# Attention scores of a hybrid decoder layer: four fp32 products of a unit replaced by twelve fp32r products of high and low parts

## The chip, the cores and the metric

One core of one Trainium2 chip runs the kernel. TensorE (PE) multiplies, VectorE (DVE), ScalarE (ACT) and GpSimd (POOL) work on the results, and SyncE's queue (SP) issues most of the DMAs. The metric is the device time of one execution in microseconds, the median of several. The kernel before took 817.43 us (3 runs, 816.8 to 818.87).

An fp32r operand is a 32-bit number that PE reads in one pass with fewer bits than fp32. The kernel gets nearly the whole precision back with a split: a number is high part plus low part, both fp32r, and a product a·b becomes the three products high·high, high·low and low·high, added up in PSUM.

## What is computed

One layer of a decoder with two branches, an mLSTM (a matrix memory, chunk by chunk) and an attention over a sliding window with sinks, for a prompt of 1024 positions and for 8 × 4 sample positions, at a width of 1024. The change is about the scores of the prompt's attention: 8 query heads in 4 groups share 2 key heads of 64 dimensions; each block of 128 positions sees its own block and the one before it.

```python
def attn_prompt(q, k, v, sinks):
    nb = T // WINDOW                                  # 8 blocks of 128
    qb = q.reshape(B, nb, WINDOW, A_HEADS, A_HEAD_DIM)
    ...
    return sink_attend(qb, with_prev(k), with_prev(v), pos, k_pos, sinks)

def sink_attend(q, k, v, q_pos, k_pos, sinks):
    s = jnp.einsum('bnqkgd,bnskd->bnkgqs', qg, k) * (A_HEAD_DIM ** -0.5)
    ...
    mx = jnp.maximum(jnp.max(s, axis=-1, keepdims=True), sink)
    p = jnp.exp(s - mx)
    den = jnp.sum(p, axis=-1, keepdims=True) + jnp.exp(sink - mx)
    o = jnp.einsum('bnkgqs,bnskd->bnqkgd', p / den, v)

def layer(...):
    (mq, mk, mv, mi, mf, mo, mz, aq, ak, av, az, gm, ga) = split_in(h @ w_in)
    y_m, C, n, m = mlstm_branch(mq, mk, mv, mi, mf, mo, mz, C0, n0, m0, b_i, b_f, g_mn)
    q, k = partial_rope(aq, pos), partial_rope(ak, pos)
    y_a = attn(q, k, av, sinks) * jax.nn.silu(az)
    u = jax.nn.sigmoid(gm) * (y_m @ w_mo) + jax.nn.sigmoid(ga) * (y_a @ w_ao)
    x = x + gate * (u @ w_o)
```

## The kernel before

The kernel goes through the layer in stages. After the norm and the split of h into high and low parts come the projections of keys, values and queries (products g_ak, g_av, g_aq, up to 125 us), then the mLSTM's heads and the gates in blocked products (bx, bw, by, bz: twelve fp32r steps of 512 columns to a block, from the high and low parts of the activations and of the weights wh and wl), then the output projections (g_w_mo, g_w_ao, foX, foY, foW).

Between the steps of these large products a planner, the class `Side`, puts the smaller work: generators in named streams, among them "a" (the attention's units), "x" (extra work, one after the other), "s" (samples) and "g" (the gates of the mLSTM). Each `yield lag, banks` of a generator says how many planned microseconds must pass before its next part and which PSUM banks that part takes. The planner's clock `now` is moved on by `mm` with each product (the matmul itself is the helper's line L292 in the profile, transposes are L297), and a bank of the pools "b" and "o" counts as taken for 3.5 and 5.5 planned us; both pools have 2 buffers. What comes out is a fixed order of PE's, DVE's and ACT's instructions (`in_order`), so any engine that waits holds up all that stands behind. DMAs go through `dma` and `store` to SP's queue (L277), in the order in which the planner reaches them; a store with `by=S` goes to ACT's queue. A tile of `ht` is one of 49 buffers of 128 × 512 numbers.

A query group's projection ends in `ev_q`, which scales a piece of 384 or 288 columns out of PSUM on ACT (aq), rotates it for group 0 and stores it to qD in DRAM. The rotated keys stand in kD, the values in vdD.

`unit(g, b0)`, 16 times (4 groups, two blocks each), is the attention. It loads the queries of two blocks into uqv (128 × 256: the two key heads' 64 rows lie one above the other) and three blocks of keys into ukv (two at b0 = 0), waits 10.0 planned us, and multiplies: for each block i and each key head a product of 64 rows, the two heads on different halves of PE's rows, into sc_.._0 (pool "o") and sc_.._1 (pool "b"). DVE adds the mask and takes the maximum in four pieces (p, mx; the custom operations of the profile), then ACT exponentiates, DVE normalises, PE transposes (pt, pool "b"), multiplies with the values (oT, pool "b"), and ACT copies oT to ukv, from where it is stored to oD.

Three other pieces of work stand near the first unit. `smp` (pool "b") are the products of the samples with raw weights wr_mv and wr_mq, as soon as these are loaded. `fp` (pool "b") is a transpose in `gates`, the chain that makes the decays nmd and wid. `ow` are the rows of w_out times the gates ogb, which are stored back to DRAM for the output projection. `sum_blocks` in stream "x" forms the sums t2, t3 and t4 of the blocks of h that the blocked products take.

Of the kernel before, what the change touches and what calls it, by code (L numbers as in the profile page):

```python
# [20 lines left out]
D = 1024  # L21
# [167 lines left out]
def body(tc, a):  # L189
    nc = tc.nc  # L190
    with ExitStack() as ctx:
# [17 lines left out]
        def ht(shape, name, dt=F32):  # L209
            return sp.tile(shape, dt, tag="half", bufs=49, name=name)  # L210
# [49 lines left out]
        def dma(out, in_, late=False):  # L260
            stores(in_.tensor)
            issue(out, in_, late)
# [25 lines left out]
        def mm(out, lhsT, rhs, start, stop, share=1, more=False):  # L288
            n = int(np.prod(rhs.shape[1:]))
            side.now += max(n, 250) / 2400 if rhs.dtype == F32R else max(n * 4 // share, 128) / 2400  # L290
            side.products += 1
            in_order(nc.tensor.matmul(out, lhsT, rhs, start=start, stop=stop, skip_group_check=more))  # L292
# [543 lines left out]
        def unit(g, b0):  # L836
            sink = at["sink"]
            los = [128 if b == 0 else 0 for b in (b0, b0 + 1)]
            n0 = 1 if b0 == 0 else 0
            qv, kv_ = ht([128, 4, 128], "uqv"), ht([128, 4, 128], "ukv")  # L840
            q, kT = qv[:, 0:2].rearrange("p c e -> p (c e)"), kv_[:, 0:3].rearrange("p c e -> p (c e)")
# [60 lines left out]
        def queries(g):  # L902

            def ev_q(p, acc, c0, n):
                q = ht([128, 384], "aq")[:, :n]
                S.activation(q, acc[:, :n], AF.Copy, scale=0.125)
                if g == 0:
                    r = ht([128, 384], "aqr")[:, :n]
                    rope(q, at["ropeq"][p], n, r, shuf16)
                    q = r  # L910
                store(qD.rearrange("g k r s -> (g k) r s")[:, 16 * g:16 * g + 16, c0:c0 + n], q)

            job(("aq", g), ev_q)

        def sample_attention():
# [12 lines left out]
            for kv, r in enumerate(half_rows):  # L928
                dma(qsm[r], qD[:, kv, :, SEQ:T].rearrange("g r s -> r g s"))
            yield 12.0, "b"  # L930
# [386 lines left out]
        def block_split(t, hi, lo):  # L1317
            S.copy(hi, t)
            V.tensor_tensor(lo, t, hi.bitcast(F32), op=ALU.subtract)

        def sum_blocks():
# [460 lines left out]
        next(work)  # L1782
        for g in range(4):
            for b0 in (0, 2, 4, 6):
                side.add("a", unit(g, b0))
# [363 lines left out]
```

## Time and profile before

| | before |
|---|---|
| median of the runs shown | 817.43 us (816.8 to 818.87, 3 runs) |
| the profiled execution | 816.73 us |
| its span on the core | 814.9 us |
| mean granted clock of TensorE | 0.998 |
| DMA, mean over the span | 193 GB/s, 157.26 MB |
| first and last query piece leave PSUM (ACT, aq) | 72.0 and 123.0 us |
| scores of the first unit | 139.1 us |
| scores of the first unit of the second group | 185.9 us |

The profile is of one execution; the page gives each engine's busy time, the chain of work that ended last and the costliest groups. In a row of a timeline stand the start, the time until the end of the last of the group, engine, line, operation, output and inputs, the tile's shape, how many, and in brackets the idle time before and what ended it. Matmuls are pipelined: the record of one is longer than the time after which the next one starts, so what a product costs PE is read from start to start.

### The profile page before, as it was taken

How to read it: one execution, taken by the hardware profiler on the slowest of the kernel's cores; microseconds unless marked ns; L12 is line 12 of the kernel's file. 1: busy time of each engine (PE TensorE's matmuls, PEld its weight loads, DVE VectorE, ACT ScalarE, POOL GpSimd, SP SyncE). 2: the span in 40 equal slices, each digit the busy share in tenths (PEclk: the TensorE clock that was granted, in tenths of full speed). 3: DMA queues.
4: the chain of work that ended last, by engine and by line, in shares of the span. 5: the costliest groups of instructions: out<-in, count | busy, mean ns of one | idle time of the engine just before them, and what ended most of it. 6: DMA issues, size and time to landing. Idle time of an engine off the chain costs nothing.

```text
span 814.9 us, 15087 instructions
## 1 busy us (share of the span) xinstructions
PE 795.6 (98%) x5071; PEld 650.3 (80%) x5071; DVE 601.2 (74%) x1631; ACT 409.2 (50%) x996; POOL 105.3 (13%) x196
## 2 busy tenths in 40 slices
PE   6899999999999999999999999999999999999996
PEld 2688887777777767887888888787788999997785
DVE  3789747989776866665766787899786677767576
ACT  4674243655646757645454655564545244215344
POOL 0220000222222220010211110111101100000041
PEclk9999999999999999999999999999999999999999
DMA  9977646878785475744364675573455698534532
GB/s 322 373 228 203 177 125 223 265 228 238 249 249 168 115 220 171 226 135 150 101 184 133 184 188 172 160 210 91 138 169 185 227 346 305 173 102 167 204 110 104
DMA packets 111041, 157.26 MB, mean 193 GB/s; under 512 B 19712, under 2 KB 61440, under 8 KB 110932
## 3 DMA queue, kind: packets, MB, share of 16 engines
q1 hardware_dynamic: 96148, 135.58, 52.5%
q10 hardware_dynamic: 11232, 14.42, 5.0%
q0 software_dynamic: 3584, 6.30, 3.9%
q8 instruction: 40, 0.66, 0.4%
q14 instruction: 37, 0.30, 0.1%
HBM read 112.58 MB, written 44.69 MB: 193 GB/s over the span
## 4 chain that ended last, share of the span: by engine, by line
PE 93%; DVE 2%; DMA 2%; ACT 1%; issue 1%; SPq 0%; ACTq 0%; DVEq 0%
PE bw L292 14%; PE by L292 13%; PE bx L292 13%; PE bz L292 7%; PE g_aq L292 6%; PE g_w_mo L292 6%; PE g_w_ao L292 5%; PE foX L292 3%; PE foW L292 2%; PE smp L292 2%; PE foY L292 2%; PE sc L292 2%; PE oT L292 2%; PE n L292 2%; PE g_ak L292 1%; PE g_av L292 1%
## 5 line engine op out<-in xcount | busy, mean ns | idle before, releaser
L273 POOL DMA_DIRECT2D yhD<-yt x48 | 28.8, 607 | 230.9 <-DVE yt L235 139.6
L292 PE MATMUL g_w_ao<-ya,wh_w_ao 128*128 128x384 f32 (+1 forms) x192 | 45.7, 322 | 0.1
L292 PE MATMUL g_w_mo<-ym_l,wh_w_mo 128*128 128x384 f32 (+1 forms) x192 | 45.7, 323 | 0.0
L235 ACT ACTIVATE p<-p,nmx 128x256 f32<-128x256 f32 (+1 forms) x64 | 31.0, 486 | 21.4 <-DVE nmx L235 20.7
L273 POOL DMA_DIRECT2D mkN<-mkt x32 | 20.9, 659 | 133.5 <-DVE p L235 71.8
L292 PEld LDWEIGHTS g_w_ao<-ya,wh_w_ao 128*128 128x128 f32 x192 | 33.5, 188 | 0.7 <-DVE ya L235 0.6
L292 PEld LDWEIGHTS g_w_mo<-ym_l,wh_w_mo 128*128 128x128 f32 x192 | 33.5, 188 | 0.0
L292 PE MATMUL g_aq<-h_h,wh_aq 128*128 128x384 f32 (+1 forms) x96 | 31.9, 333 | 0.0
L292 PE MATMUL g_aq<-h_l,wh_aq 128*128 128x384 f32 (+1 forms) x96 | 31.0, 323 | 0.0
L292 PE MATMUL g_w_mo<-ym_l,wl_w_mo 128*128 128x384 f32 (+1 forms) x96 | 31.0, 323 | 0.0
L292 PE MATMUL g_aq<-h_h,wl_aq 128*128 128x384 f32 (+1 forms) x96 | 31.0, 323 | 0.0
L292 PE MATMUL g_w_ao<-ya,wl_w_ao 128*128 128x384 f32 (+1 forms) x96 | 30.8, 321 | 0.0
L235 ACT CAST uwh<-u_h 128x512 fp32r<-128x512 f32 x27 | 16.6, 620 | 27.3 <-PE foY L292 10.5
L235 DVE TENSOR_TENSOR uwl<-u_h,uwh 128x512 fp32r<-128x512 f32 x27 | 18.5, 689 | 12.5 <-ACT uwh L235 12.4
L235 DVE CUSTOM_DVE_ANT_0 p<-sc,cst,sink 128x256 f32<-128x256 f32 (+1 forms) x64 | 26.1, 461 | 1.0 <-PE sc L292 1.0
L273 POOL DMA_DIRECT2D mvN<-mvt x32 | 20.7, 653 | 37.3 <-DVE mvt L235 36.3
L235 ACT CAST wo_h<-wo_l 128x512 fp32r<-128x512 f32 x28 | 17.1, 620 | 13.8 <-DVE u_h L235 10.6
L235 POOL TENSOR_TENSOR fr_w<-fr_y 128x2 f32<-128x2 f32 (+1 forms) x12 | 3.5, 291 | 144.2 <-DVE fr_y L235 143.6
L235 ACT ACTIVATE p<-p,den 128x128 f32<-128x128 f32 x56 | 18.6, 394 | 5.1 <-DVE den L235 4.5
L235 DVE TENSOR_TENSOR wo_l<-wo_l,wo_h 128x512 fp32r<-128x512 f32 x28 | 18.7, 686 | 2.5 <-ACT wo_h L235 2.4
L235 DVE SCALAR_TENSOR_TENSOR p<-p,den 128x128 f32<-128x128 f32 x56 | 17.3, 345 | 4.2 <-ACT wh_pgate__3658 L235 2.9
L292 PEld LDWEIGHTS g_aq<-h_h,wh_aq 128*128 128x128 f32 x96 | 18.0, 188 | 2.7 <-issue 2.5
(1621 smaller groups left out, 2684.3 us busy)
## 6 DMA issues: line engine op xcount, KB each, us to landing
x<-xT SPq DMA_DIRECT2D x16, 256.0 KB
early_h<-w_ada SPq DMA_DIRECT2D x8, 512.0 KB
adar_ga<-w_ada SPq DMA_DIRECT2D x16, 256.0 KB
ow<-w_out SPq DMA_DIRECT2D x16, 256.0 KB
woD_t<-ow SPq DMA_DIRECT2D x16, 256.0 KB
wr_ga<-w SPq DMA_DIRECT2D x16, 256.0 KB
wr_gm<-w SPq DMA_DIRECT2D x16, 256.0 KB
taD<-gt ACTq DMA_DIRECT2D x16, 256.0 KB
```

Of the source, the lines that this page charges most:

```text
L235: ins = f(*args, **kw)
L273: nc.gpsimd.dma_start(out, in_)
L292: in_order(nc.tensor.matmul(out, lhsT, rhs, start=start, stop=stop, skip_group_check=more))
```

## The change

The queries leave PSUM in two parts: ACT writes the high part (fp32r), DVE the difference; for group 0 both are taken after the rotation. They are stored to qhD and qlD, and the 32 sample columns, unsplit, to qsD, from where `sample_attention` reads them. A new generator `key_parts` in stream "x" loads the rotated keys from kD once, splits them and stores khD and klD. `unit` loads four pieces in place of two (queries high and low into one uqv, keys into ukh and ukl), passes them through ACT in three copies in place that give them the type fp32r, and forms each block's scores from three products; the output goes to a part of p. The lag of 10.0 before the scores becomes 8.0 and, after the copies, 2.5. `sum_blocks` begins with a yield of 6.0, and the planner's cost of an fp32r product is divided by its share.

```diff
-            side.now += max(n, 250) / 2400 if rhs.dtype == F32R else max(n * 4 // share, 128) / 2400
+            side.now += max(n, 250) / share / 2400 if rhs.dtype == F32R else max(n * 4 // share, 128) / 2400
...
-        qD = dp.tile([4, 2, 64, T], F32, name="qD")
+        qD = [dp.tile([4, 2, 64, SEQ], F32, name=f"q{x}D") for x in "hl"]
+        qsD = dp.tile([4, 2, 64, NS], F32, name="qsD")
+        ksD = [dp.tile([128, SEQ], F32, name=f"k{x}D") for x in "hl"]
...
         def unit(g, b0):
-            qv, kv_ = ht([128, 4, 128], "uqv"), ht([128, 4, 128], "ukv")
-            q, kT = qv[:, 0:2]..., kv_[:, 0:3]...
-            dma(q, qD[g].rearrange("k r s -> (k r) s")[:, b0 * 128:b0 * 128 + 256])
-            dma(kT[:, n0 * 128:], kD[:, (b0 - 1 + n0) * 128:(b0 + 2) * 128])
-            yield 10.0, "obt"
+            qv = ht([128, 4, 128], "uqv", F32R)
+            q = [qv[:, 2 * i:2 * i + 2].rearrange("p c e -> p (c e)") for i in range(2)]
+            kT = [ht([128, 512], f"uk{x}", F32R)[:, :384] for x in "hl"]
+            for t, d in zip(q, qD):
+                dma(t.bitcast(F32), d[g].rearrange("k r s -> (k r) s")[:, b0 * 128:b0 * 128 + 256])
+            for t, d in zip(kT, ksD):
+                dma(t[:, n0 * 128:].bitcast(F32), d[:, (b0 - 1 + n0) * 128:(b0 + 2) * 128])
+            yield 8.0, ""
+            for t in (qv, kT[0][:, n0 * 128:], kT[1][:, n0 * 128:]):
+                S.copy(t, t.bitcast(F32))
+            yield 2.5, "obt"
...
-                for kv, r in enumerate(half_rows):
-                    mm(scs[kv][:, i, lo:], q[r, qc], kT[r, kc], start=True, stop=True, share=2)
+                for j, (x, y) in enumerate(((0, 0), (0, 1), (1, 0))):
+                    for kv, r in enumerate(half_rows):
+                        mm(scs[kv][:, i, lo:], q[x][r, qc], kT[y][r, kc], start=(j == 0), stop=(j == 2), share=2)
...
-            o = kv_[:, 0:2].rearrange("p c e -> p (c e)")
+            o = p[0][:, 0]
...
             def ev_q(p, acc, c0, n):
-                q = ht([128, 384], "aq")[:, :n]
-                S.activation(q, acc[:, :n], AF.Copy, scale=0.125)
+                parts = [ht([128, 384], f"aq{x}", F32R)[:, :n] for x in "hl"]
+                hi, lo = parts
                 if g == 0:
...
+                    rope(t, at["ropeq"][p], n, q, shuf16)
+                    S.copy(hi, q)
+                    V.tensor_tensor(lo, q, hi.bitcast(F32), op=ALU.subtract)
+                else:
+                    S.activation(hi, acc[:, :n], AF.Copy, scale=0.125)
+                    V.scalar_tensor_tensor(lo, acc[:, :n], 0.125, hi.bitcast(F32), op0=ALU.mult, op1=ALU.subtract)
...
+        def key_parts():
+            raw, hi, lo = ([ht([128, 512], f"ks{x}", dt) for _ in range(2)] for x, dt in ...)
+            for i in range(2):
+                dma(raw[i], kD[:, HALF[i]])
+            yield 6.0, ""
+            for i in range(2):
+                block_split(raw[i], hi[i], lo[i])
+                for t, d in zip((hi[i], lo[i]), ksD):
+                    store(d[:, HALF[i]], t.bitcast(F32))
+                yield 2.0, ""
+
         def sum_blocks():
...
+            yield 6.0, ""
...
         for g in (1, 0, 2):
             queries(g)
+        side.add("x", key_parts())
```

Since the planner sets the order, all work after about 130 us is laid out anew. Two places are shown.

The first is the first unit. PE, in the kernel before, where the sample products end and the unit's scores follow (by and bx are blocked products of the heads, wh and wl their weights):

```order
L292 MATMUL smp<-wr_mq_0_1512,c_106 32x128
L292 MATMUL smp<-wr_mq_1_1514,c_106 32x128
L292 MATMUL sc_0_0_1650<-ukv,uqv 128x128
L292 MATMUL sc_0_1_1651<-ukv,uqv 128x128
L292 MATMUL sc_0_0_1650<-ukv,uqv 128x256
L292 MATMUL sc_0_1_1651<-ukv,uqv 128x256
L292 MATMUL bx<-h_h_388,wh_phead_in_1__1579 128x512
```

The same engine and place after the change, from the last of the unit's scores on:

```order
L292 MATMUL sc_0_1_1710<-ukl,uqv 128x256
L292 MATMUL sc_0_0_1709<-ukh,uqv 128x256
L292 MATMUL sc_0_1_1710<-ukh,uqv 128x256
L297 MATMUL fp<-cst,gt_1120 128x32
L292 MATMUL by<-t3h_1482,wh_phead_in_7__1631 128x512
L292 MATMUL by<-t3l_1483,wh_phead_in_7__1631 128x512
L292 MATMUL by<-t3h_1482,wl_phead_in_7__1632 128x512
L292 MATMUL smp<-wr_mv_0_1574,c_106 32x128
```

The sixteen smp products stood ahead of the scores and now stand behind them, behind fp and behind three steps of by that were ahead of smp before.

DVE at this place, in the kernel before: the products of w_out's rows with the gates, one sum of raw weights, and the first of the unit's four pieces.

```order
L235 TENSOR_TENSOR ow_1536<-ow_1536,ogb_1532 128x512
L235 TENSOR_TENSOR ow_1538<-ow_1538,ogb_1533 128x512
L235 TENSOR_TENSOR ow_1540<-ow_1540,ogb_1532 128x512
L235 TENSOR_TENSOR wr_mq_0_1512<-wr_mv_0_1508,wr_mq_0_1512 128x512
L235 TENSOR_TENSOR ow_1542<-ow_1542,ogb_1533 128x512
L235 ISA p_1647,mx<-sc_0_0_1650,cst,sink 128x128
```

After the change:

```order
L235 TENSOR_TENSOR ow_1604<-ow_1604,ogb_1600 128x512
L235 TENSOR_TENSOR t4l_1620<-x_7_86,t4h_1619 128x512
L235 TENSOR_TENSOR ow_1606<-ow_1606,ogb_1601 128x512
L235 TENSOR_TENSOR ow_1608<-ow_1608,ogb_1600 128x512
L235 TENSOR_TENSOR ow_1610<-ow_1610,ogb_1601 128x512
L235 ISA p_1706,mx<-sc_0_0_1709,cst,sink 128x128
```

Four products ow and one other operation stand ahead of the pieces in both; the other one is now the low part of a sum (t4l), and the sum of raw weights comes behind the pieces. On SP's queue the loads of ow come after the weights wr_mv and wr_mq in both orders. Between them stood one load of ogb; now the loads of the low queries, of both parts of the keys and of two ogb stand there.

The second place is the unit sc_4 of the last group, at 301 to 306 us in the trace. DVE in the kernel before, from the multiplication of the decays et to the unit's first piece:

```order
L235 TENSOR_TENSOR et<-et,cst 128x384
L235 SCALAR_TENSOR_TENSOR p_3458<-p_3459,den 128x128
L235 TENSOR_TENSOR wl_pgate_3__3618<-wr_ga_1_3085,wh_pgate_3__3617 128x512
L235 TENSOR_TENSOR wl_pgate_4__3659<-wr_gm_1_3089,wh_pgate_4__3658 128x512
L235 TENSOR_TENSOR wr_gm_0_3439<-wr_ga_0_3435,wr_gm_0_3439 128x512
L235 TENSOR_TENSOR qw<-qw,hq_0_3547 128x384
L235 TENSOR_TENSOR wr_ga_0_3435<-ws_3612,wr_ga_0_3435 128x512
L235 ISA p_3596,mx<-sc_4_0_3599,cst,sink 128x256
```

After the change:

```order
L235 MEMSET hv_0_3824 128x3
L235 SCALAR_TENSOR_TENSOR p_3736<-p_3737,den 128x128 x2
L235 TENSOR_TENSOR et<-et,cst 128x384
L235 TENSOR_TENSOR wr_gm_0_3694<-wr_ga_0_3690,wr_gm_0_3694 128x512
L235 TENSOR_TENSOR wl_pgate_3__3903<-wr_ga_1_3306,wh_pgate_3__3902 128x512
L235 ISA p_3873,mx<-sc_4_0_3876,cst,sink 128x256
```

One wl, qw and the second sum of raw weights (wr_ga) now come behind the pieces.

More of the change, by code (lines that the diff above doesn't have):

```diff
@@ L902, in queries @@
         def queries(g):
+            rows = [d.rearrange("g k r s -> (g k) r s")[:, 16 * g:16 * g + 16] for d in (*qD, qsD)]
             def ev_q(p, acc, c0, n):
[L905 to L906 removed]
+                parts = [ht([128, 384], f"aq{x}", F32R)[:, :n] for x in "hl"]
+                hi, lo = parts
+                m = min(n, SEQ - c0)
                 if g == 0:
[L908 to L911, printed above, removed]
+                    q, t = (ht([128, 384], f"aqr{x}")[:, :n] for x in "qt")
+                    S.activation(t, acc[:, :n], AF.Copy, scale=0.125)
+                    rope(t, at["ropeq"][p], n, q, shuf16)
+                    S.copy(hi, q)
+                    V.tensor_tensor(lo, q, hi.bitcast(F32), op=ALU.subtract)
+                    tail = q[:, m:]
+                else:
+                    S.activation(hi, acc[:, :n], AF.Copy, scale=0.125)
+                    V.scalar_tensor_tensor(lo, acc[:, :n], 0.125, hi.bitcast(F32), op0=ALU.mult, op1=ALU.subtract)
+                    if m < n:
+                        tail = sm([128, NS], "aqs", 2)
+                        S.activation(tail, acc[:, m:n], AF.Copy, scale=0.125)
+                for t, d in zip(parts, rows):
+                    store(d[:, :, c0:c0 + m], t[:, :m].bitcast(F32))
+                if m < n:
+                    store(rows[2], tail)
             job(("aq", g), ev_q)
@@ L1319, in block_split @@
             V.tensor_tensor(lo, t, hi.bitcast(F32), op=ALU.subtract)
+        def key_parts():
+            raw, hi, lo = ([ht([128, 512], f"ks{x}", dt) for _ in range(2)] for x, dt in (("r", F32), ("h", F32R), ("l", F32R)))
+            for i in range(2):
[6 more added lines that the diff above has]
+                yield 2.0, ""
         def sum_blocks():
@@ L1782, in body @@
         next(work)
+        assert not side.streams["x"]["wait"] and len(side.streams["x"]["live"]) < 2
         for g in range(4):
```

4 lines of the change are left out of this document (2 added, 2 removed).

## The prediction

> **What bounds the kernel now.** The page comes first: who is busy, and what the chain that ended last is made of. Then the list of all the waits of TensorE (PE).
>
> ```profile
> span 814.9 us, 15087 instructions
> ...
> PE 795.6 (98%) x5071; PEld 650.3 (80%) x5071; DVE 601.2 (74%) x1631; ACT 409.2 (50%) x996; POOL 105.3 (13%) x196
> ...
> PE 93%; DVE 2%; DMA 2%; ACT 1%; issue 1%; SPq 0%; ACTq 0%; DVEq 0%
> ```
>
> ```profile
> PE xc L292 <- ACT xsq L235: 5.8, 1, 5.8
> PE pt L297 <- DVE mx L235: 2.3, 1, 2.3
> PE adat_q L292 <- ACT adas_q L235: 1.5, 2, 0.8
> PE xc L292 <- ACT xsum L235: 0.7, 1, 0.7
> PE bw L292 <- ACT bw L235: 0.7, 1, 0.7
> PE g_av L292 <- DVE wl_av L235: 0.6, 1, 0.6
> PE g_ak L292 <- DVE h_l L235: 0.5, 1, 0.5
> ```
>
> PE is busy for 98% of the span and makes up 93% of the chain. The list (us in all, times, longest) has seven kinds of wait, 12 us together, and one of them lies in the attention: 2.3 us, in which PE's transposes of the probabilities (pt) wait for VectorE (DVE). So a microsecond taken from PE's instruction stream between 137 and 310 us is a microsecond of the end, and so is each new wait of PE there; work on ScalarE (ACT), DVE or the queues costs something only where it makes PE wait.
>
> All sums below are made against the profiled execution, 816.73 us (span 814.9). The median of the runs shown is 817.43, 0.70 above it; I add that at the end. About 0.3%, 2.5 us, is what a measurement of this kernel can tell from no change: 815.0 to 819.9.
>
> **The scores (12 products for 4).** What one unit costs PE is read from start to start in PE's timeline, for the two kinds of unit.
>
> ```profile
> 175.32 0.40 PE L292 MATMUL bw<-h_h,wl_phead_in__2009 128*128 128x512 f32 x1
> 175.64 1.13 PE L292 MATMUL sc<-ukv,uqv 64*128 64x256 f32 x8
> 176.71 0.66 PE L297 MATMUL pt<-cst,p 128*128 128x128 f32 x4
> ```
>
> ```profile
> 137.78 0.39 PE L292 MATMUL by<-t3h,wl_phead_in__1559 128*128 128x512 f32 x1
> 138.10 0.30 PE L292 MATMUL smp<-wr_mv,c 128*32 128x128 f32 x2
> ...
> 139.11 0.93 PE L292 MATMUL sc<-ukv,uqv 64*128 64x128 f32 x8
> 139.96 0.50 PE L292 MATMUL bx<-h_h,wh_phead_in__1579 128*128 128x512 f32 x1
> ```
>
> A unit of two full blocks takes 176.71 − 175.64 = 1.07 us, a first unit of a group (its first block has 128 keys) 139.96 − 139.11 = 0.85. The eight records of a unit are four matmuls in two passes, and the two matmuls of a pair lie in different halves of the rows, so there are four pair passes, two for each block. The two kinds differ by 0.22 in two passes of 128 columns, 0.11 each; a pass of 256 is then 0.22, the four 0.87, and 0.20 is left for going into and out of the half-height tiles. What an fp32r step of 256 columns takes, the end of the kernel shows.
>
> ```profile
> 802.00 0.28 PE L292 MATMUL foY<-wo_h,uwh 128*128 128x256 f32 x1
> ...
> 807.63 0.28 PE L292 MATMUL foY<-wo_h,uwl 128*128 128x256 f32 x1
> ```
>
> These are 48 rows: (807.63 − 802.00) / 47 = 0.120 us a step. Six pair steps are 0.72 instead of 0.87: **−0.15 us in each of 12 units, −1.8 us**. An fp32r step of 128 columns on half the rows stands nowhere; it lies between 0.06 (half of 0.12) and 0.12 (no cheaper than 256 columns), so a first unit's six steps are 3 × 0.06 to 3 × 0.12 and 3 × 0.12, 0.54 to 0.72, where its four passes were 0.65; I take 0 for the four. The 0.20 of overhead I keep. An fp32r product on 96 rows passes without any (0.23 a step on both sides of it),
>
> ```profile
> 596.27 0.40 PE L292 MATMUL sU<-vm,skn 96*128 96x512 f32 x1
> 596.50 0.40 PE L292 MATMUL bw<-t2h,wh_phead_gate__7130 128*128 128x512 f32 x1
> ```
>
> so the overhead's bounds are 0 and 0.20, and the scores' term lies between −1.8 and −1.8 − 16 × 0.20 = −5.0; I stay near the 64-row rows, since they are the same tiles. If the two halves ran in turn, the twelve steps would be 1.44: a rival, below.
>
> The Trainium skill (TensorEngine Tiling (Array Packing), Instruction Overhead) gives each matmul about 60 cycles of overhead on this chip and advises against tiling what is already small, which speaks against more and shorter products; with the 2.4 GHz of its page TensorE: Matmul & The Clock Gate that would be an estimated 25 ns a step, some 0.05 us for the two added steps of a unit and about 1 us for the kernel. The 256-column steps above show 120 ns, only 13 above 256 such cycles, so the trace bears out about half of it, and that half is in the 0.72 already.
>
> **A new wait at the first unit.** The order of PE changes at about 138 us: the first unit's scores, the transposes fp and one block's three products now come ahead of the sample products smp, where smp came before the scores. The half of the scores on the second key head (sc_0_1), fp and smp share a pool of two banks, so smp now takes the bank of sc_0_1 and waits until DVE has read it. When that is, DVE's timeline tells.
>
> ```profile
> 137.56 2.04 DVE L235 TENSOR_TENSOR ow<-ow,ogb 128x512 f32<-128x512 f32 x3 [0.95 <-DMA ow<-w_out]
> 139.52 0.69 DVE L235 TENSOR_TENSOR wr_mq<-wr_mv,wr_mq 128x512 f32<-128x512 f32 x1
> 140.12 0.69 DVE L235 TENSOR_TENSOR ow<-ow,ogb 128x512 f32<-128x512 f32 x1
> 140.73 0.35 DVE L235 CUSTOM_DVE_ANT_0 p<-sc,cst,sink 128x128 f32<-128x128 f32 x1
> ...
> 142.08 0.09 DVE L235 DVE_READ_ACCUMULATOR2_ANT mx<- 128x1 f32 x1
> 142.95 0.24 PE L297 MATMUL fp<-cst,gt 32*128 32x32 f32 x1
> ```
>
> The reads end at 142.17, and nothing of PE waits for them now. In the new order PE gets to smp at 138.10 (where it stood) + 0.85 (the scores) + about 0.35 (fp, 0.24 and the change of tiles) = 139.3; the three products are moved, not added. That leaves 142.17 − 139.3 = **2.9 us of wait**. Behind smp in PE's queue stands everything, so it goes to the end in full. And DVE gets there later: its pieces p still stand behind four products ow and one more operation of 0.69 us, and the ow loads now stand on SP's queue behind 512 KB more since the weights (a second ogb, and the new low parts of queries and keys). At the rate of that stretch,
>
> ```profile
> 125.00:140.00 15.00, 14.34 (x97) 11.01 (x96) 10.13 (x24) 6.82 (x16) 0.00 (x0) 1.00 0.75 249
> 140.00:180.00 40.00, 40.00 (x238) 30.67 (x237) 36.57 (x109) 21.75 (x62) 9.90 (x16) 1.00 0.79 249
> 180.00:220.00 40.00, 40.00 (x276) 30.83 (x275) 31.54 (x87) 24.83 (x73) 10.98 (x18) 1.00 0.84 250
> ...
> 260.00:310.00 50.00, 47.74 (x338) 36.09 (x338) 35.51 (x114) 33.98 (x108) 10.33 (x16) 1.00 0.57 171
> ```
>
> 249 GB/s (the last column; ahead of it the DMA share, the clock and the busy times of PE, its loads, DVE, ACT and POOL), this is 2.1 us. DVE was itself waiting 0.95 us for ow there, so a later landing is not hidden. I take half: **+4.0**; the ends are +2.0 (the loads land in time and the pieces move up by the 0.95 us) and +5.5 (all of the 2.1, and one more operation of DVE ahead).
>
> **The wait at 306 us.** Before pt, DVE works through a row of 0.6 us products that begin with a late load.
>
> ```profile
> 300.98 0.56 DVE L235 TENSOR_TENSOR et<-et,cst 128x384 f32<-128x384 f32 x1 [1.06 <-DMA et<-nmd]
> ...
> 302.32 0.69 DVE L235 TENSOR_TENSOR wl_pgate__3659<-wr_gm,wh_pgate__3658 128x512 fp32r<-128x512 f32 x1
> ...
> 303.52 0.55 DVE L235 TENSOR_TENSOR qw<-qw,hq 128x384 f32<-128x384 f32 x1
> ...
> 306.35 0.66 PE L297 MATMUL pt<-cst,p 128*128 128x128 f32 x4 [2.26 <-DVE mx L235]
> ```
>
> In the new order three of them (a wl, qw and a wr_ga, 0.6 us each) come behind the pieces that lead to pt. That is 1.8 of the 2.26 us; but pt's place on PE moves too, and the load of et sits on the same queue with more ahead of it. I take **−1.2**, ends −2.3 and 0.
>
> **ACT, DVE and the queues.** Each unit adds three casts on ACT; each query piece adds a product on DVE.
>
> ```profile
> L235 ACT CAST h_h<-x 128x512 fp32r<-128x512 f32 x12 | 7.1, 621 | 0.3
> L235 ACT CAST ya<-yr 128x384 fp32r<-128x384 f32 x8 | 3.9, 508 | 0.0
> L235 DVE SCALAR_TENSOR_TENSOR u_h<-tgw_ao,g_w_ao 128x384 f32<-128x384 f32 x16 | 8.7, 550 | 6.2 <-PE g_w_ao L292 6.1
> 100.00:125.00 25.00, 25.00 (x184) 22.05 (x183) 10.76 (x25) 9.61 (x20) 0.00 (x0) 1.00 0.39 107
> ```
>
> A unit costs ACT 0.62 + 2 × 0.51 = 1.64 us, 16 units 26 us, in a stretch of 185 us where it was busy for 108 (the sum of the windows; 68% in the last, 260 to 310). The cover is ACT's idle 40%, and the unit's lag before the scores (8.0 + 2.5 planned microseconds for 10.0). Twelve query pieces are 12 × 0.55 = 6.6 us of DVE, half of them in 100 to 125, where it is idle for 14 of 25; key_parts adds two casts (1.2) and two subtractions (1.4) there. Bytes: 16 units × 320 KB, 1.5 MB for key_parts, and 2 MB of query stores, some 8.5 MB where the DMA share is 0.39 to 0.84. Where this cover is gone PE waits; I take **+0.4**, ends 0 and +4.
>
> **Sum**: 816.73 − 1.8 + 4.0 − 1.2 + 0.4 = 818.1, and 0.7 for the median: 818.8; I take off 0.2, since the unknown overhead of the tiles can only fall: **818.6**, by this sum no change that can be told.
>
> **The rivals.**
>
> *The wait stays short and the tile change shrinks.* For it: sU's step without overhead, and DVE's idle 0.95 us. Scores −4.0 (two thirds of the overhead gone), smp +2.0, pt −2.0, nothing else: 817.43 − 4.0 = 813.4. Against it: the 0.20 is measured on these very tiles, and the reads by DVE do end at 142.17. The Trainium skill (TensorEngine Tiling (Array Packing), Key Properties) says that changing the tiling mode drains TensorE; by that rule the overhead stays, and the rows of sc agree with 0.20 us, while sU at 96 rows shows none.
>
> *ACT becomes late (slower).* One mechanism: ACT runs in order, and 1.64 us of casts stand ahead of its next evacuation of a product block. In 260 to 310 four units bring 6.6 us to 33.98, 81% of the stretch. A block's twelve steps take 12 × 0.23 = 2.8 us, and with two banks PE waits as soon as ACT is later than that. For it: the wait bw <- ACT bw, 0.7 us, is of this kind. Against it: ACT's idle time there is still 9 us. Where each of the four costs 1 us: +4 on the forecast, 822.5.
>
> *The pairs run in turn.* The scores then don't get cheaper: 1.44 − 0.87 = +0.57 in 12 units, 6.8, and in the others, between 1.1 and 1.4 for 0.65, +0.6 in 4, 2.4: together +9.2 where the sum has −1.8. That is 11 on the forecast, of which 0.6 shortens the wait at smp: about 829. For it: no fp32r pair on half-height tiles stands in the trace. Against it: the fp32 pairs, in the same tiles, do run side by side.
>
> **How the numbers follow.** Forecast 0.48 (its own range 816.5 to 821), shorter wait 0.26 (813.4, ± 2), ACT late 0.16 (822.5, ± 2.5), pairs in turn 0.10 (829). Faster than 815.0: 0.20 of the second and 0.02 of the first, 0.22. Slower than 819.9: 0.13 of the first, 0.13 of the third and 0.10 of the fourth, 0.36. The rest, 0.42, is within. The range 812.5 to 825.0 leaves out the fourth (0.10), the lowest part of the second (0.05) and the top of the third (0.04).
>
> **What would show it.** PE's timeline at a full unit: 0.92 from the scores' start to the next one's (0.87 or less if the overhead shrinks, 1.6 if in turn). In the list of waits: smp <- DVE p or mx with 3 to 5 us near 139, once; pt <- DVE mx below 1.5 us; nothing <- ACT longer than 1 us in 140 to 310. ACT's busy time about 437. The prediction is wrong if smp isn't waiting at all, or if a wait of PE that the list doesn't have now comes with every unit.

## The result, and the profile after

The changed kernel takes 827.58 us (median of 4 runs, 827.48 to 829.85), the kernel before beside it 817.12 (4 runs): a ratio of 1.0135, 95% interval 1.0112 to 1.0158. That is 10.5 us slower, where 818.6 was forecast with 825.0 as the upper end. The profiled execution took 829.85 us and its span is 827.7, 12.8 longer than that of before.

The page after, the same lines as before the change: the busy times and what the chain is made of.

```profile
span 827.7 us, 15375 instructions
...
PE 797.1 (96%) x5135; PEld 653.5 (79%) x5135; DVE 610.1 (74%) x1645; ACT 432.9 (52%) x1052; POOL 105.2 (13%) x196
...
PE 76%; DVE 10%; DMA 6%; ACT 4%; issue 2%; SPq 1%; ACTq 0%; DVEq 0%
```

PE is busy 1.5 us longer, and the rest of the 12.8 is standstill. Its share of the chain fell from 93% to 76%; DVE, DMA and ACT took it. The list of PE's waits (us in all, times, longest), from its longest down:

```profile
PE xc L292 <- ACT xsq L235: 6.6, 1, 6.6
PE smp L292 <- DVE mx L235: 5.7, 1, 5.7
PE smp L292 <- ACT p L235: 2.7, 1, 2.7
PE adat_q L292 <- ACT adas_q L235: 1.5, 2, 0.8
PE smpo L292 <- DVE mx L235: 1.4, 1, 1.4
...
PE pt L297 <- DVE mx L235: 0.4, 1, 0.4
```

All 16 entries come to 23.4 us, where it was 12.1. The first, xc, is the first product of all; in the profiles of this case it waits 5.8 to 7.5 us, whatever the edit, so its 0.8 us more is not put down to the change. The wait of pt that the prediction spoke of is gone (the 0.4 of pt in this list is another one, at 227 us), but three new ones stand there, of smp and smpo, 9.8 us together.

**The scores.** PE's timeline at a full unit:

```profile
184.76 0.38 PE L292 MATMUL sc<-ukh,uqv 64*128 64x256 f32 x2
184.98 0.28 PE L292 MATMUL sc<-ukl,uqv 64*128 64x256 f32 x2
...
185.45 0.28 PE L292 MATMUL sc<-ukh,uqv 64*128 64x256 f32 x2
185.66 0.50 PE L292 MATMUL by<-t4h,wh_phead_in__2156 128*128 128x512 f32 x1
```

From 184.76 to 185.66 are 0.90 us, where four fp32 products took 1.07; 0.92 was forecast. Ten of the twelve full units take 0.90 or 0.91 us; the last two, at 314 and 322 us, take about 1.1, and the four first units 0.89 where it was 0.85. Together the scores cost PE 1.4 us less. The next product after the first pair starts 0.22 later, and from the second pair (184.98) to the last (185.45) four steps take 0.47, 0.12 each: the halves run side by side.

**The first unit.** PE there, and DVE:

```profile
140.49 0.40 PE L292 MATMUL by<-t3h,wl_phead_in__1632 128*128 128x512 f32 x1
146.59 0.43 PE L292 MATMUL smp<-wr_mv,c 128*32 128x128 f32 x2 [5.71 <-DVE mx L235]
```

```profile
142.09 0.69 DVE L235 TENSOR_TENSOR ow<-ow,ogb 128x512 f32<-128x512 f32 x1 [4.03 <-DMA ow<-w_out]
142.70 0.68 DVE L235 TENSOR_TENSOR t4l<-x,t4h 128x512 fp32r<-128x512 f32 x1
143.30 1.89 DVE L235 TENSOR_TENSOR ow<-ow,ogb 128x512 f32<-128x512 f32 x3
145.10 0.34 DVE L235 CUSTOM_DVE_ANT_0 p<-sc,cst,sink 128x128 f32<-128x128 f32 x1
...
146.46 0.08 DVE L235 DVE_READ_ACCUMULATOR2_ANT mx<- 128x1 f32 x1
```

DVE stands still for 4.03 us until the first load of ow has landed, goes through four ow and t4l, and only then reads the scores; the read of the last piece ends at 146.54 and PE's smp starts at 146.59. The queue's timeline shows why the load is late, before the change and after it:

```profile
131.14 1.85 SPq L277 DMA_DIRECT2D ow<-w_out  x4
```

```profile
134.96 2.81 SPq L277 DMA_DIRECT2D ow<-w_out  x4
```

The four loads are issued 3.8 us later. Most of that is there before the loads that the change adds at this place: the store of gb (gbD), which stands ahead of them on the queue, is 3.5 us later already. Before and after:

```profile
125.15 0.24 SPq L277 DMA_DIRECT2D gbD<-gb  x1
```

```profile
125.65 1.30 SPq L277 DMA_DIRECT2D qlD<-aql  x1
127.04 0.57 SPq L277 DMA_DIRECT2D qsD<-aqs  x1
127.67 0.45 SPq L277 DMA_DIRECT2D uqv<-qhD  x1
128.21 0.38 SPq L277 DMA_DIRECT2D wr_mv<-w  x1
128.69 0.24 SPq L277 DMA_DIRECT2D gbD<-gb  x1
```

DVE finishes gb 1.8 us later than before (126.93 us for 125.12), and the queue is then still at the stores of the query parts and two loads. From the store of gb to the loads of ow it is 6.0 us before and 6.3 after, so the added loads between them hardly count.

And something comes after the wait that no step of the prediction has. The windows around it (PE, its loads, DVE, ACT, POOL, then the granted clock, DMA share and GB/s):

```profile
142.00:144.00 2.00, 0.00 (x0) 0.00 (x0) 1.91 (x4) 0.00 (x0) 0.00 (x0) 1.00 1.00 330
144.00:146.00 2.00, 0.00 (x0) 0.00 (x0) 2.00 (x7) 1.12 (x3) 0.00 (x0) 0.64 0.93 298
146.00:148.00 2.00, 1.41 (x28) 1.32 (x32) 1.40 (x8) 1.59 (x7) 0.00 (x0) 0.50 0.74 211
148.00:150.00 2.00, 2.00 (x16) 1.32 (x9) 1.42 (x4) 1.36 (x6) 0.00 (x0) 0.50 0.94 327
150.00:152.00 2.00, 2.00 (x8) 1.57 (x7) 1.31 (x5) 1.68 (x5) 0.00 (x0) 0.65 0.29 105
```

While PE stands still its granted clock falls to half, and it comes back only at about 151.4 us. The products from 146.6 to 151.4 take about 2.3 us longer than at full clock.

So the 12.8 us of the two spans are: waits +11.3 (23.4 − 12.1), low clock +2.3, scores −1.4, and 0.6, on balance, in the spacing of other products.

**Near 310 us.** Where pt waited, smp now does. The rows of DVE, ACT and PE, in order of time:

```profile
309.26 0.69 DVE L235 TENSOR_TENSOR ws<-wr_gm,wr_gm 128x512 f32<-128x512 f32 x1 [4.54 <-DMA wr_gm<-w]
309.87 0.16 DVE L235 TENSOR_SCALAR nmx<-mx 128x4 f32<-128x4 f32 x1
```

```profile
310.06 0.51 ACT L235 ACTIVATE p<-p,nmx 128x256 f32<-128x256 f32 x1 [3.52 <-DVE nmx L235]
```

```profile
313.06 0.30 PE L292 MATMUL smp<-wr_ga,c 128*32 128x128 f32 x2 [2.73 <-ACT p L235]
```

On DVE a sum of raw weights (ws) stands ahead of the unit's nmx and waits 4.54 us for its weights; ACT's exponentials wait for nmx, and PE waits for a bank of pool "b" that ACT empties behind them, with the copy of oT to p:

```profile
312.66 0.35 ACT L235 COPY p<-oT 128x256 f32<-128x256 f32 x1
```

### The profile page after: what moved, and what is told of

It reads as the page before. It is cut to its first block, busy times and chain, and to the rows that moved or that the text cites. A ratio compares the mean times of both kernels' runs of the same rounds, so it can differ in the third digit from the quotient of the medians.

```text
span 827.7 us, 15375 instructions
## 1 busy us (share of the span) xinstructions
PE 797.1 (96%) x5135; PEld 653.5 (79%) x5135; DVE 610.1 (74%) x1645; ACT 432.9 (52%) x1052; POOL 105.2 (13%) x196
## 4 chain that ended last, share of the span: by engine, by line
PE 76%; DVE 10%; DMA 6%; ACT 4%; issue 2%; SPq 1%; ACTq 0%; DVEq 0%
PE by L292 11%; PE bw L292 11%; PE bx L292 11%; PE bz L292 6%; PE g_w_mo L292 6%; PE g_w_ao L292 5%; PE g_aq L292 3%; PE foX L292 3%; PE foW L292 2%; PE foY L292 2%; PE smp L292 2%; ACT p L235 2%; PE n L292 2%; DVE p L235 2%; DMA ow<-w_out 1%
## 5 line engine op out<-in xcount | busy, mean ns | idle before, releaser
L235 ACT CAST uwh<-u_h 128x512 fp32r<-128x512 f32 x27 | 16.6, 619 | 27.4 <-PE foY L292 10.5
L235 DVE TENSOR_TENSOR h_l<-x,h_h 128x512 fp32r<-128x512 f32 x20 | 13.8, 691 | 7.2 <-ACT h_h L235 5.9
```

Of the source, the lines that this page charges most:

```text
L235: ins = f(*args, **kw)
```

## The experiments

Times are medians beside runs of the kernel before on the same chip, whose median in these calls was 816.6 to 817.3 us.

| run | median us | ratio to before, 95% |
|---|---|---|
| changed kernel | 827.58 | 1.0135 (1.0112 to 1.0158) |
| e1 PE kept busy in the wait | 826.31 | 1.0119 (1.0087 to 1.0150) |
| e2 fp32 scores | 829.12 | 1.0153 (1.0129 to 1.0177) |
| e3 ow products later | 825.70 | 1.0114 (1.0087 to 1.0140) |
| e4 ow products behind the first unit | 824.22 | 1.0086 (1.0055 to 1.0117) |
| e5 no casts | 830.70 | 1.0147 (1.0105 to 1.0189) |
| e6 = e4 and e5 | 821.76 | 1.0047 (1.0025 to 1.0070) |
| e7 = e6 without low loads | 821.03 | 1.0043 (1.0024 to 1.0063) |
| e9 = e6, sums of weights behind nmx | 820.08 | 1.0041 (1.0021 to 1.0060) |
| e10 = e6, keys' subtractions on POOL | 822.20 | 1.0065 (1.0042 to 1.0089) |
| e11 = e9 and e10 | 820.24 | 1.0044 (1.0024 to 1.0064) |
| e16 = e9, query stores on POOL's queue | 820.42 | 1.0039 (1.0022 to 1.0056) |
| e12 sum_blocks without its yield | 837.79 | 1.0244 (1.0212 to 1.0275) |
| e8 before + loads and casts | 822.88 | 1.0064 (1.0036 to 1.0092) |
| e13 before + loads | 823.14 | 1.0067 (1.0043 to 1.0091) |
| e14 before + casts | 816.79 | 0.9991 (0.9976 to 1.0005) |
| e15 before + preparation | 831.45 | 1.0174 (1.0148 to 1.0200) |
| e17 before, query stores on POOL's queue | 816.08 | 0.9991 (0.9977 to 1.0006) |

**e1: PE kept busy in the first wait.**

```diff
-            fp = pb([128, 128], "fp")
+            fp = pb([128, 512], "fp")
+            bh = blocks["b11"][0][0]
+            for _ in range(31):
+                in_order(nc.tensor.matmul(fp[:, 128:512], bh[:, :128], bh[:, :384], start=True, stop=True, ...))
```

> The changed kernel with 31 products of 384 columns added ahead of fp at the first unit; they go to unused columns of fp's bank, and nothing reads them. They take 31 x 0.16 = 5.0 us of the 5.7 us that PE stands still before smp, so smp starts when it did. Theory (PE's granted clock of 0.5 from 145 to 151 us comes from the standstill, and costs the end 2.3 us): the wait falls to about 0.7 us, the steps after it are 0.23 us, not 0.43, and the time is 827.6 - 2.3 = 825.3. Rival (the low clock has another cause, or later waits take its cost up): 827.6, with the clock as low as before in the first case and whole in the second.

In its trace the wait of smp for mx is gone from the list, and the clock is 1.00 in all windows from 138 to 310 us; the time is 1.3 us less than the changed kernel's, with intervals that overlap. That the standstill makes the clock fall is shown. What it is worth at the end is not told to the microsecond, because in this profiled execution the clock fell after the wait at 309 us instead (0.50 from 313 to 316 us), where it had not in the changed kernel's.

**e2: fp32 scores.**

```diff
-                for j, (x, y) in enumerate(((0, 0), (0, 1), (1, 0))):
-                    for kv, r in enumerate(half_rows):
-                        mm(scs[kv][:, i, lo:], q[x][r, qc], kT[y][r, kc], start=(j == 0), stop=(j == 2), share=2)
+                then = side.now + 3 * 2 * max(256 - lo, 250) / 2 / 2400
+                for kv, r in enumerate(half_rows):
+                    mm(scs[kv][:, i, lo:], q[0][r, qc].bitcast(F32), kT[0][r, kc].bitcast(F32), start=True, stop=True, share=2)
+                side.now = then
```

> The changed kernel with the scores formed as before the change, four fp32 products a unit, from the high parts alone: the low parts are loaded, cast and not used. The planner's clock moves as in the changed kernel, and PE's order is the same but for the scores. Theory (the scores' term of the prediction holds, -1.8 us, and PE's stream sets the end): 827.6 + 1.8 = 829.4, full units 1.07 us from start to start for 0.92. Rival (the term is hidden by waits behind it): 827.6 within 0.5. Second rival (the twelve products are the loss): 820 or less.

The copy of fp on DVE is also tied behind the first unit's pieces, where it stands in the changed kernel. The unit that took 0.90 us takes 1.06 from start to start:

```profile
184.50 1.14 PE L292 MATMUL sc<-ukh,uqv 64*128 64x256 f32 x8
185.56 0.50 PE L292 MATMUL by<-t4h,wh_phead_in__2132 128*128 128x512 f32 x1
```

The median is 1.5 us higher, near the 1.8 expected and the 1.4 of the trace, though the intervals overlap. The twelve products are not the loss; that rival falls.

**e3 and e4: the first wait taken away.** In e3 the first lag of out_weights is 11.0; e4 has this too, and the DVE products ow of the first four loads are also tied behind the first unit's four pieces.

```diff
-                yield 7.0, ""
+                yield 7.0 if ks[0] else 11.0, ""
                 for j, t in enumerate(ts):
-                    V.tensor_tensor(t, t, gb[j % 2], op=ALU.mult)
+                    scaling = V.tensor_tensor(t, t, gb[j % 2], op=ALU.mult)
+                    if ks[0] == 0:                                  # e4
+                        no_sync(getattr(scaling, "ins", scaling), pieces[:4])
```

> The changed kernel with the first lag of the ow products 11.0 instead of 7.0; PE's order is unchanged. On DVE the copy of fp now stands behind the first ow and t4l alone, ahead of the others and of the unit's pieces, and smp takes fp's bank instead of that of the scores. Theory (smp waits for what DVE does behind the first ow load, landed at 142.1, and the clock falls only in a long standstill): smp at 143.6, a wait of 2.7 us instead of 5.7, clock whole, 827.6 - 3.0 - 2.3 = 822.3. Rival (the clock falls in any standstill of over 2 us): 824.6. Second rival (the gain is given back at later waits): above 826.

> As e3, and the ow products of the first four rows come behind the first unit's pieces on DVE; the copy of fp has no ow ahead of it. PE's order is unchanged. Theory (the late ow load in DVE's queue is the whole cause of the wait at smp): no wait over 0.5 us there, clock whole, 827.6 - 5.7 - 2.3 = 819.6. Rival (the later waits at 310 us grow by what is won, since they hang on loads): 823 to 826.

e3's wait is 2.2 us, where 2.7 was expected, but its clock falls all the same. PE stops at 139.9 us, and the windows of one microsecond show the clock at half from 141.2, 1.2 us later, until 148:

```profile
140.00:141.00 1.00, 0.00 (x0) 0.00 (x0) 0.33 (x1) 0.86 (x2) 0.00 (x0) 1.00 1.04 402
141.00:142.00 1.00, 0.00 (x0) 0.00 (x0) 1.00 (x4) 0.00 (x0) 0.00 (x0) 0.58 1.07 389
...
147.00:148.00 1.00, 1.00 (x4) 0.71 (x4) 0.18 (x2) 0.95 (x5) 0.00 (x0) 0.51 0.75 280
```

So a standstill of 2.2 us can be enough, as e3's rival has it; but not any of over 2 us is, since the clock stayed whole at 2.3 us in the kernel before and at 2.7 near 310 us in the changed one. e4 has no wait at smp there, its clock is 1.00 from 125 to 260 us, and its span is 821.3, 6.4 less than the changed kernel's; the ow loads at the head of DVE's queue were the cause of the first wait. But its median is 824.2, 4.6 above what was expected and within its rival's 823 to 826, and 7 us stay. The rival's reason is half right: the wait of smp near 305 us did not grow (2.2 us), but now the clock falls there, to half from 305.9 to 309.4 us.

**e5 to e7: ACT's casts, and the bytes of the low parts.** e5 drops the three `S.copy` of a unit, e6 is e4 with e5, e7 drops the loads of the low parts as well; all its twelve products take the high parts, so its scores leave the low parts out.

> The changed kernel without the three casts in place of each unit (the parts are stored rounded, so the numbers are the same); PE's order is unchanged, ACT has 51 instructions and some 26 us less. Theory (the later waits come from loads that DVE waits for, ACT only passes them on): the wait smp <- ACT p near 313 us stays above 1.5 us, the wait at the first unit stays near 5.7, 827.6 - 1 = 826.6. Rival (ACT has become late, as the prediction's second rival has it): the waits for ACT and for p and mx after 220 us go, 822 to 823.5.

> e4 (the ow products of the first four rows behind the first unit's pieces on DVE) and e5 (no casts) together. Theory (the casts cost 1 us at most): 824.2 - 1 = 823.2, waits of PE for smp and smpo after 270 us as in e4. Rival (ACT late): 819 to 820.

> e6 without the loads of the low parts: two loads a unit instead of four, 320 KB less each, and all twelve products take the high parts. Theory (bytes and issues on the queue make the weights wr_gm land late, for which DVE stands still ahead of the unit's nmx): DVE's waits for wr_gm shrink from some 7 us to under 3, PE's waits near 278 and 303 us together from 3.6 to under 1.5, the clock falls less, 823.2 - 3.5 = 819.7. Rival (the loads are late for another cause, the order in which they are issued): within 1 of e6.

e5 is no faster, and its waits are the same (smp <- DVE mx 5.5, smp <- ACT p 3.2): ACT passes the delay on and does not make it. e6 came out 1.4 below the 823.2 expected. e7 is within 0.7 of e6, so its rival holds: the bytes of the low parts are not what the mended kernel loses by.

**e9 to e11 and e16: the places that were left.** e9 ties each sum of weights behind the latest nmx, e10 moves two subtractions to POOL, e11 does both, e16 issues the query parts' stores from POOL's queue.

```diff
+                sums = V.tensor_tensor(self.raw["s1"], self.raw[1, 0], self.raw[1, 1], op=ALU.add)   # e9
+                no_sync(getattr(sums, "ins", sums), bounds)
...
-                    store(d[:, :, c0:c0 + m], t[:, :m].bitcast(F32))
+                    scatter(d[:, :, c0:c0 + m], t[:, :m].bitcast(F32))                               # e16
```

> e6, and on DVE every sum of raw weights (ws, which waits for its weights' load) stands behind the nmx of the unit begun last. PE's order is unchanged. Theory (near 278 and 303 us PE waits because ws, waiting for wr_gm, stands ahead of nmx on DVE, and ACT's exponentials and the copies behind them wait for nmx): PE's waits for smp <- ACT p and smpo <- DVE mx, together 4.0 us in e6, fall under 1.5, with them the low clock behind the first, 821.8 - 3 = 818.8. Rival (PE then waits for the weights themselves, a little later): within 1 of e6.

> e6, with key_parts' two subtractions on POOL, which is idle there, instead of DVE. PE's order is unchanged. Theory (the changed kernel is 1.3 us behind at 125 us because DVE, busy without a gap from 117 to 128, reaches the chain gp, gb, bq late): two thirds of DVE's delay there go, 821.8 - 0.8 = 821.0, the waits gp <- adas_ga and bq <- gb under 0.3. Rival (the delay comes from loads): no change there.

> e9 and e10 together: the change with the first unit's pieces ahead of the ow products, no casts, the sums of weights behind nmx and the keys' subtractions on POOL. Theory: 818.8 - 0.8 = 818.0, level with the kernel before (817.2) within 0.3%; what is left is 3 us less in the scores and pt than the sum of what loads and DVE still cost. Rival (the traffic costs wherever it is put, as in e8): 821 to 823.

> e9, with the stores of the queries' high and low parts issued from POOL's queue, which is idle there, not from SP's. The order of PE, DVE and ACT is unchanged. Theory (the stores' issue on SP delays the weights' loads by 3 us and so costs what e9 is behind at 125 us): the load of wr_mq is issued some 3 us earlier, ACT's wait for it (4.7 us in the changed kernel) falls under 2.5, 820.1 - 1.3 = 818.8, level with the kernel before. Rival (what is left comes from the units' loads, as in e13): within 0.7 of e9.

In e9 the waits of smp and smpo are gone, so the sums were their cause. The median is 1.7 lower than e6's, about half of what was expected, and the intervals overlap. The old wait of pt is back, and longer, and behind it the clock is at half from 308.3 to 311.8 us:

```profile
PE pt L297 <- DVE mx L235: 3.5, 1, 3.5
```

e10 won nothing: in its trace PE waits 2.6 us for aql and 1.7 for adas_ga in the very place. e11 is as e9. In e16 ACT's wait for wr_mq is no longer listed, yet the time is that of e9. None of the mended kernels is level with the kernel before.

**e12: sum_blocks at once.** The changed kernel without the new `yield 6.0`.

> The changed kernel without the new yield of 6.0 at the start of sum_blocks; all else of the change is in. By the planner's clock the sample products smp then stand ahead of the first unit's scores again, as before the change, and wait for no bank that DVE holds. Theory (the swap of smp and the scores is what costs the 5.7 us and the low clock, and it comes from this one line): no wait at smp near 140 us, 827.6 - 5.7 - 2.3 = 819.6, plus up to 3 for waits behind 270 us that come with the loads. Rival (the standstill comes with the late ow loads in any order): a wait of 4 us or more on another tile there, 825 to 828.

This theory fell. There is indeed no wait at smp near 140 us, so the swap of smp and the scores does come with that line, but the kernel is 10 us slower than the changed one. Its first product bx of the heads starts at 129.44 us, where it is 125.27 in the kernel before and 126.55 in the changed one, and nine times between 82 and 240 us more than 1 us lies between the starts of two products (once in the kernel before). The line hides more than it costs.

**e8, e13 to e15 and e17: the parts of the added work alone, on the kernel before.** e8 adds a second load of queries and keys and three copies on ACT to each unit, e13 the loads alone, e14 copies alone (four, of the queries and the keys twice each); e15 adds the split of queries and keys and the stores of their parts, beside the whole store of before.

```diff
             dma(q, qD[g].rearrange("k r s -> (k r) s")[:, b0 * 128:b0 * 128 + 256])
+            dma(qv[:, 2:4].rearrange("p c e -> p (c e)"), qD[g]...)                       # e8, e13
             dma(kT[:, n0 * 128:], kD[:, (b0 - 1 + n0) * 128:(b0 + 2) * 128])
+            dma(ukl[:, n0:3].rearrange("p c e -> p (c e)"), kD[:, ...])                   # e8, e13
-            yield 10.0, "obt"
+            yield 8.0, ""
+            for t in (qv, kv_[:, n0:3], ukl[:, n0:3]):                                    # e8
+                S.copy(t, t)
+            yield 2.0, "obt"
```

> The kernel before, and each unit loads its queries and keys a second time (320 KB, two more loads) and passes all of it through ACT in three copies in place; the second halves are not used, scores and their precision are as before. The planner's lag stays 10.0 in sum, and PE's order changes in 24 rows of its 3834. Theory (the traffic of the units costs by itself, whatever the order): +2 to +4, 819 to 821, with new waits of PE behind DVE's waits for weights after 270 us. Rival (the loss is all in the new order): 816.9 within 0.7.

> The kernel before, and each unit loads its queries and keys a second time (two more loads, 320 KB), unused; no casts. Theory (loads that come late for DVE are the cost): most of e8's 5.7 us, 820.5 to 822, with the waits pt <- DVE mx as in e8. Rival (the casts are the cost): 817.3 within 1.

> The kernel before, and each unit passes its queries (twice) and its keys through ACT in three copies in place; no more loads. Theory (loads are the cost): 817.3 within 1. Rival (casts): 820.5 to 822, with waits of PE for ACT or for what follows ACT's exponentials.

> The kernel before, and the queries and keys are split and their parts stored as in the change (twelve and two products on DVE, casts on ACT, 31 more DMAs), unused; queries and keys are also stored whole as before. PE's order is unchanged. Theory (the preparation costs what the changed kernel is behind at 125 us): +1.3 to +2.0, 818.6 to 819.3, in waits for gp, bq and g_aq before 130 us. Rival (hidden, as the prediction has it, 0.4 for all of ACT, DVE and queues): 817.3 within 0.7.

> The kernel before, with the query stores issued from POOL's queue. PE's and DVE's order is unchanged. Theory (nothing waits for these stores' queue before the change): 817.1 within 0.7. Rival (the same gain is there without the change): 816 or less.

The casts cost nothing (0.9991): ACT's idle time covers them, as the prediction said. The loads cost 6.0 us (e13), all of what e8 cost. The lag split in two (8.0 and 2.0 for 10.0) also moves some scores and transposes in PE's order, in e13 and e14 alike, and e14 shows that this costs nothing. In e13's trace an example stands at 166 us, DVE first, then PE:

```profile
166.47 0.69 DVE L235 TENSOR_TENSOR ow<-ow,ogb 128x512 f32<-128x512 f32 x1 [2.10 <-DMA ow<-w_out]
167.08 0.48 DVE L235 CUSTOM_DVE_ANT_0 p<-sc,cst,sink 128x256 f32<-128x256 f32 x1
```

```profile
168.84 0.66 PE L297 MATMUL pt<-cst,p 128*128 128x128 f32 x4 [2.49 <-DVE mx L235]
```

It is the pattern of the first unit again: a load that comes late, an operation of DVE that waits for it, the pieces behind that, and PE behind their bank. This traced execution took 820.75 us, 2.4 less than the median, and its two waits of pt come to 3.8 us where the kernel before has 2.3, so it shows this pattern for a part of the 6.0 only. In e8's trace, with the same loads (823.77 us), they come to 5.3 us, and the clock is at half from 170.4 to 173.9 behind the first.

The preparation alone costs 14.3 us (e15), far above the 1.3 to 2.0 expected. Its queue and ACT, from the last query store ahead of the weights on:

```profile
112.54 1.01 SPq L277 DMA_DIRECT2D qlD<-aql  x1
113.65 0.87 SPq L277 DMA_DIRECT2D m_p<-scratch  x1
114.57 1.77 SPq L277 DMA_DIRECT2D wr_mq<-w  x2
```

```profile
118.89 0.62 ACT L235 CAST wh_phead_in__1586<-wr_mq 128x512 fp32r<-128x512 f32 x1 [6.91 <-DMA wr_mq<-w]
```

SP needs about 0.6 to 1.0 us for the issue of each such store, so three for one push back the loads of the weights behind them (in the kernel before the first is issued at 106.80 us). ACT stands 6.91 us at the cast of these weights, and the evacuation of g_aq stands behind the cast. The bank's second reader, DVE's aql, comes at 123.05 us, behind a sum of weights that DVE begins only at 122.44; PE waits 4.1 us for that bank. Further on pt waits 3.8 us, and the clock is at half from 67.8 to 71.3, 122.5 to 129.4 and 177.1 to 184.0 us, so waits (+7.9 us in the list) and low clock share the loss in about equal parts. e17 shows that the kernel before loses nothing by its own query stores on that queue.

The changed kernel has a wait of ACT for wr_mq too, of 4.7 us. That the 1.3 us by which it is behind at 125 come from there is not shown: in e16 that wait is gone, and the first product bx starts at 127.05 us, in e9 at 125.78; counted from the first product g_aq it is 60.9 us for 61.1.

## Why the prediction was wrong

Against the span of before the sum forecast +1.4 us (818.1 − 816.73), and the trace has +12.8. Term by term: the wait at the first unit +5.7 for +4.0, the waits near 286 and 310 us +1.8 for −1.2, the low clock +2.3 where the sum had no term, all other waits but xc +3.0 for +0.4, the scores −1.4 for −1.8; xc and the spacing of other products make up the rest.

**What bounds the kernel** was right: what was taken from PE's stream came out of the end, and each wait of PE went in.

**The scores, −1.8**, were right in their mechanism and nearly in size: −1.4 in the trace. The pairs run side by side, with the 0.20 of overhead that was kept (0.90 − 6 × 0.12 = 0.18). What is missing is in the first units, taken as 0, where a step of 128 columns takes 0.11 us, hardly less than one of 256, and in the last two units; why those are longer was not found. The rival of pairs in turn, whose 829 is nearest to the time measured, is wrong. The Trainium skill (TensorEngine Tiling (Array Packing), Key Properties) has a change of the tiling mode drain TensorE; the trace agrees, with about 0.2 us for each unit before and after.

**The new wait at the first unit, +4.0**, was right in its place, its chain (bank, pieces, ow, load) and its sign, and too small: 5.7, above its upper end of 5.5. I priced the lateness of the ow loads by bytes over the stretch's mean rate and took half of it, about 1 us. The bytes were also 640 KB, not 512, since the high part of the keys stands there too. But the loads were issued 3.8 us later, and 3.5 of that came from further up the queue, with the late store of gb behind the stores of the query parts; I had looked only at what stands between the weights and ow. PE, then 1.3 us behind, was at smp at 140.9, not 139.3.

**No term for the clock.** A wait of PE was priced at its length. The standstill halved the granted clock until 151.4, which adds 2.3 us. No row of before showed that, since its waits inside the stretch were 2.3 us at most and the clock stood at 1.00 there.

**The wait at 306 us, −1.2**, was right for the instruction named (the 2.3 us of pt there are gone) and wrong for the end: smp waits 2.7 and smpo 1.4 in its place, because ws with a late load stands ahead of nmx. The question that the prediction put, what is late next, I answered only for the three operations that moved.

**ACT, DVE and the queues, +0.4**, is the step that failed most by its reasoning. ACT's part was right (e14: nothing). But the loads and the stores were counted as bytes against a share of 0.39 to 0.84. Added alone to the kernel before, the loads cost 6.0 us and the preparation 14.3, each beyond the upper end of 4 that I gave for all of it. (e15 stores three parts of each query piece on SP's queue, the change two, so its 14.3 is more than the change can owe to them.) In-order engines wait for one late load each, and that does not show in a mean share.

The rival that came nearest in its mechanism was named for the wrong engine: ACT does stand late, but it passes on what DMA and DVE hold up, and taking its work away (e5) changes nothing.

Open: with both long standstills mended (e9, e16) the kernel is still 0.4% behind the kernel before. In e9's trace the wait of pt and the low clock behind it are most of that; in e16's pt waits 1.9 us, the clock stays whole, and the rest is spread over many small waits. The parts' costs do not add up either: 6.0 and 14.3 alone, 10.5 together with the line that mends some of it, and e7 shows no gain from fewer bytes. What of the last 3 us belongs to which load was not found.

## What to carry to other kernels

Price an added DMA on a shared queue by the next loads behind it, from the first place where the queue falls behind, and follow each of those to the in-order engine whose next instruction waits for it; bytes over mean bandwidth say little. Where a planner reorders, ask of each pool of two banks which reader now stands between two users, and allow for a stretch at half clock behind a wait of PE of 2 us or more. A saving of 2 us on the bounding engine that needs 8 MB of extra traffic in a stretch with a DMA share of 0.8 has to show first where the traffic waits.

## What the runs showed of the hardware

The clock falls after standstills as short as 2.0 us (e12: PE resumes at 171.5, at half from 172.4 to 175.9) and 2.2 us (e3: stopped at 139.9, at half from 141.2 to 148), but not after each: the 2.7 us at 310 in the changed kernel left it at 1.00, and the 2.5 us at the same place in e1 halved it from about 312.7 to 316. Once it fell with no wait of PE ahead (e15, 67.8 to 71.3, after 2 us of products of 8 columns). Each stretch at half clock ahead of the last products lasted 3.4 or 6.8 us. The Trainium skill (TensorE: Matmul & The Clock Gate, What's actually happening) has a free-running window of about 3.4 us and an idle window before the clock falls; the lengths here agree with one and two such windows, while a fall 1.2 us after the stop does not fit a whole idle window.

Between the starts of two pairs of fp32r products of 64 rows lie 0.11 us at 128 columns (the first unit, 139.02 to 139.13) and 0.12 at 256 (a full unit, 0.47 in four steps), so the shorter ones save next to nothing.

The issue of a DMA is no constant: a store of a query part (128 rows of 384 or 288 numbers into a strided place) holds SP's queue for 0.57 to 1.30 us in the changed kernel, a unit's load of queries for 0.32 to 0.88.
